# A two-layer decoder trunk: in the MLP's first iteration, casts move to GpSimd and modulation rows start one iteration later

## Chip, cores, metric

One core of one Trainium2 chip runs the whole trunk in one launch. The metric is the device time of one execution in microseconds (us), the median of several runs.

## The reference, cut to what matters

The trunk has two layers. Each has a mixer and then a squared-ReLU MLP, and each of these four sublayers is wrapped in the same way: normalise, scale and shift by rows computed from `c`, apply, normalise, gate, add. The change touches the two MLPs alone.

```python
def squared_relu_mlp(h, w1, w2):
    return jnp.square(jax.nn.relu(h @ w1)) @ w2          # (1024,1024) @ (1024,4096) @ (4096,1024)

def sandwich(x, c_act, sublayer, g_pre, g_post, w_mod, b_mod):
    shift, scale, gate = jnp.split(c_act @ w_mod + b_mod, 3, axis=-1)   # w_mod: 1024 x 3072
    h = rms_norm(x, g_pre) * (1 + scale[:, None]) + shift[:, None]
    return x + gate[:, None] * rms_norm(sublayer(h), g_post)
```

All data are float32, batch 1, 1024 tokens, width 1024.

## The kernel before

**Products in three passes.** A float32 operand is split into two parts: a "high" part, cast to the type fp32r, and a "low" part, the operand minus the high part. A product then takes three matmul passes (high x high, high x low, low x high). `split_w` (L153) makes both parts of a weight block of 128x1024: the cast runs on ScalarE (L160), the subtraction on VectorE (L162, both of its inputs in SBUF). If the counter `spare` is above zero, `split_w` takes one off it and casts on GpSimd instead (L158). `split_to` (L499) does the same for other operands: the cast on ScalarE (L500), the subtraction on VectorE (L501).

**The MLP's first product** (`h @ w1`) is done with seven products of half-size blocks in place of eight (Strassen's scheme in Winograd's form). Tokens are split in two halves, and the width and the hidden columns likewise. There are eight iterations `it` over hidden columns. Each loads four weight blocks x11, x12, x21, x22 (L579), forms sums of them on VectorE (L615 to L618, L628), and issues products number 1, 2, 4, 6, 7, 5, 3 in that order on TensorE (L547 to L549, called at L606 to L645), each with its own `split_w`. One iteration has 7 x 2 x 12 matmuls of 128x512. Six PSUM banks serve the products.

**Iteration 0 has more to do.** The first token half arrives in split form from the sublayer before. The second half is made inside iteration 0, after products 1 and 2, by `second_half` (L551). For each of four k it transposes two blocks on TensorE (L564), scales and shifts them on ScalarE (L566, L568), forms a high part's low part (L570) and four sums on VectorE (L571 to L574, two SBUF inputs each), and splits the four sums with `split_to` (L575, L576): 16 casts of 128x512 on ScalarE and 16 subtractions on VectorE. Products 4, 6, 7, 5 and 3 read these. Just before, the sublayer that precedes still finishes its last token tiles: `post` (L374: L380 to L390) and `pre_norm` (L367: square on ScalarE L370, mean on VectorE L133, power on GpSimd L135, scaling on VectorE L372), on which the transposes L564 wait.

**Modulation rows.** The queue `bgq` holds tasks that load 128 rows of `w_mod` (L285, a transfer issued on SyncE's queue) and accumulate them on VectorE (L287 for the first of eight, L289 for the others, 128x1024). Every eighth task also ends a row (`fin`: splits it, multiplies it with ones on TensorE, L306 or L323, and so on). In the MLP, each iteration but the first pops up to four tasks (L661 to L663). The first MLP has 24 tasks, so iterations 1 to 6 take them; the second has 8, taken in iterations 1 and 2.

**What sets the order.** Instructions are written in program order, but a planner then orders each engine's instructions by priority (earlier in the program goes first) and by the times at which it expects them to be ready. On the chip each engine runs its list strictly in that order, so an instruction that waits holds up everything behind it on its engine.

Of the kernel before, what the change touches and what calls it, by code (L numbers as in the profile page):

```python
# [28 lines left out]
def trunk(ctx: ExitStack, tc: tile.TileContext, x, c, rel_bias, norm_gains, mod_w, mod_b, mlp_w1, mlp_w2,  # L29
          e_w_in, e_conv_w, e_conv_b, e_dt_bias, e_A_log, e_D, e_ssd_norm, e_lambda, e_diff_norm, e_w_out,  # L30
          o_w_in, o_sinks, o_w_out, k_mat, k_onehot, k_mask, k_rope, k_ret, out, subs=(0, 1, 2, 3)):
    nc = tc.nc
# [27 lines left out]
    def turn(i):  # L60

        turns[i] = 1 - turns.get(i, 1)
        return turns[i]
# [87 lines left out]
    spare, lo_on = [0], [nc.vector]  # L151
# [262 lines left out]
    def new_hT(hf):  # L414
        return tuple(hp.tile([P, 8, 512], F32R, tag=f"{n}{hf}", name=f"{n}{hf}") for n in ("hh", "hl"))
# [80 lines left out]
                    hT[1] = make_hT(yp, 1, s + 1)  # L496
                return second

    def split_to(hi, lo, src):  # L499
        nc.scalar.copy(out=hi, in_=src)  # L500
        nc.vector.tensor_tensor(out=lo, in0=src, in1=hi.bitcast(F32), op=ALU.subtract)  # L501

    def mlp(yp, s):
# [13 lines left out]
        def bank():  # L517
            at[0] += 1
            return pg.tile([P, 512], F32, tag="g", name="pg") if at[0] % 6 < 2 else pw("pw")
# [3 lines left out]
        with ExitStack() as st:  # L523
            cp = st.enter_context(pool("c", 2))

            def block(tag):
                return cp.tile([P, 512], F32, tag=tag, name=tag)


            def pieces(i):  # L530
                return [slot(i + n, [P, 2, 512], F32R, "s") for n in range(2)]

            def of(t2):
                return lambda k: t2[k // 2][:, k % 2]

            def cols_of(t, k0):
                return lambda k: t[:, k0 + k]

            hh0, hl0 = hT[0]
            A = {1: (cols_of(hh0, 0), cols_of(hl0, 0)), 2: (cols_of(hh0, 4), cols_of(hl0, 4))}  # L540
# [10 lines left out]
            def second_half():  # L551
                a, b = mcol[s]
                hh1, hl1 = new_hT(1)
                A[4] = (cols_of(hh1, 4), cols_of(hl1, 4))
                A[7] = (cols_of(hh1, 0), cols_of(hl1, 0))
                for i, at_ in ((6, 8), (5, 4), (3, 0)):
                    A[i] = (of(pieces(at_)), of(pieces(at_ + 2)))
                for k in range(4):
                    a11, a12 = yp.whole[k], yp.whole[k + 4]
                    a2 = []  # L560
                    for kk, tag in ((k, "u3"), (k + 4, "c21")):
                        ps = pt.tile([P, 512], F32, tag="t", name="pht")
                        for i in range(4):
                            nc.tensor.transpose(ps[:, i * P:(i + 1) * P], yp.Y[4 + i][:, kk * P:(kk + 1) * P], ident)  # L564
                        a2.append(block(tag))
                        nc.scalar.activation(a2[-1], ps, AF.Identity, scale=a[:, kk:kk + 1], bias=b[:, kk:kk + 1])  # L566
                        if kk >= 4:
                            nc.scalar.activation(hh1[:, kk], ps, AF.Identity, scale=a[:, kk:kk + 1], bias=b[:, kk:kk + 1])  # L568
                    a21, a22 = a2
                    tt(out=hl1[:, k + 4], in0=a22, in1=hh1[:, k + 4].bitcast(F32), op=sub)  # L570
                    tt(out=a11, in0=a11, in1=a21, op=sub)  # L571
                    tt(out=a21, in0=a21, in1=a22, op=add)
                    tt(out=a22, in0=a22, in1=a11, op=sub)
                    tt(out=a12, in0=a12, in1=a22, op=sub)  # L574
                    for i, src in ((6, a22), (7, a11), (5, a21), (3, a12)):  # L575
                        split_to(A[i][0](k), A[i][1](k), src)  # L576

            def load(it):
                c0 = it * 256  # L579

                def src(j, r0, r1):
                    return w1[r0:r1, j * 2048 + c0:j * 2048 + c0 + 256].rearrange("(k p) n -> p k n", p=P)
                one = wp.tile([P, 8, 256], F32, tag="raw", name="raw", bufs=2)
                nc.sync.dma_start(out=one, in_=src(0, 0, D))
                if it == 0:
                    two = wp.tile([P, 8, 256], F32, tag="raw", name="raw", bufs=2)
                    nc.sync.dma_start(out=two, in_=src(1, 0, D))
                    two = [two[:, 0:4], two[:, 4:8]]
                else:
                    two = [slot(12 + i, [P, 4, 256], F32, "raw2") for i in range(2)]  # L590
                    for i in range(2):
                        nc.sync.dma_start(out=two[i], in_=src(1, i * 512, i * 512 + 512))
                return one[:, 0:4], two[0], one[:, 4:8], two[1]
# [3 lines left out]
            def square_relu(t, src):  # L597
                nc.scalar.activation(t, src, AF.Relu)
                nc.scalar.activation(t, t, AF.Square)

            for it in range(8):
                x11, x12, x21, x22 = load(it)
                pa, p1 = [bank(), bank()], [block("p1") for _ in range(2)]
                w = split_w(shape, x11)
                for g in range(2):
                    product(pa[g], 1, w, g, True, True)  # L606
                    nc.scalar.copy(out=p1[g], in_=pa[g])
                w = split_w(shape, x21)
                c11 = [block("c11") for _ in range(2)]
                for g in range(2):  # L610
                    product(pa[g], 2, w, g, False, True)
                    square_relu(c11[g], pa[g])
                if it == 0:
                    second_half()
                tt(out=x11, in0=x12, in1=x11, op=sub)  # L615
                t2 = slot(16, shape, F32, "t2")
                tt(out=t2, in0=x22, in1=x11, op=sub)
                tt(out=x21, in0=x21, in1=t2, op=sub)  # L618
                w = split_w(shape, x21)
                pe = [bank(), bank()]  # L620
                for g in range(2):
                    product(pe[g], 4, w, g, True, True)
                w = split_w(shape, t2)
                pb = [bank(), bank()]
                for g in range(2):
                    product(pb[g], 6, w, g, True, True)
                    tt(out=p1[g], in0=pb[g], in1=p1[g], op=add)
                tt(out=x12, in0=x22, in1=x12, op=sub)  # L628
                w = split_w(shape, x12)
                pc_ = [bank(), bank()]  # L630
                u3, c21 = [block("u3") for _ in range(2)], [block("c21") for _ in range(2)]
                for g in range(2):
                    product(pc_[g], 7, w, g, True, True)
                    tt(out=u3[g], in0=pc_[g], in1=p1[g], op=add)
                    tt(out=c21[g], in0=pe[g], in1=u3[g], op=add)
                    square_relu(c21[g], c21[g])
                w = split_w(shape, x11)
                pd = [bank(), bank()]
                for g in range(2):
                    product(pd[g], 5, w, g, True, True)  # L640
                    tt(out=u3[g], in0=pd[g], in1=u3[g], op=add)
                    square_relu(u3[g], u3[g])
                w = split_w(shape, x22)
                for g in range(2):
                    product(pd[g], 3, w, g, False, True)  # L645
                    tt(out=p1[g], in0=pd[g], in1=p1[g], op=add)
                    square_relu(p1[g], p1[g])
                sums = [slot(17 + i, [P, 2, 512], F32, "sums") for i in range(3)]
                for g in range(2):
                    kt = 2 * it + g  # L650
                    nc.sync.dma_start(out=ud[1][kt], in_=c11[g])
                    nc.sync.dma_start(out=ud[4][kt], in_=u3[g])
                    tt(out=sums[0][:, g], in0=c21[g], in1=u3[g], op=add)
                    tt(out=sums[1][:, g], in0=sums[0][:, g], in1=c11[g], op=sub)
                    tt(out=c21[g], in0=c11[g], in1=c21[g], op=sub)
                    nc.sync.dma_start(out=ud[7][kt], in_=c21[g])
                    tt(out=sums[2][:, g], in0=p1[g], in1=sums[1][:, g], op=sub)
                    nc.sync.dma_start(out=ud[2][kt], in_=p1[g])
                for i, n in ((5, 0), (6, 1), (3, 2)):
                    nc.sync.dma_start(out=ud[i][2 * it:2 * it + 2].rearrange("k p n -> p k n"), in_=sums[n])  # L660
                if it:  # L661
                    for _ in range(min(4, len(bgq))):
                        bgq.popleft()(slot(14 + turn(14), [P, D], F32, "mraw"))  # L663

# [939 lines left out]
```

## Time and profile before

| | us |
|---|---|
| median of 3 runs | 3015.42 |
| lowest, highest run | 3014.13, 3019.18 |
| the profiled execution, its device time | 3012.64 |
| its span, first to last instruction | 3010.7 |
| TensorE busy in the span | 2927.7 |
| VectorE busy | 1992.1 |
| ScalarE busy | 1320.9 |
| GpSimd busy | 443.5 |

The profile calls the engines PE (TensorE matmul), PEld (its weight load), DVE (VectorE), ACT (ScalarE), POOL (GpSimd) and SP (SyncE's queue). "L500" is line 500 of the kernel. PEclk is the granted TensorE clock as a share of full speed. The first MLP's iteration 0 lies at about 1084 to 1141 us of the span, the second one's about 1270 us later, with nearly the same times.

### The profile page before, as it was taken

The numbers are of one execution on the slowest core, as the hardware profiler recorded it, in microseconds if no ns is written. First come the engines' busy times: TensorE is split into PE (matmuls) and PEld (weight loads), VectorE is DVE, ScalarE is ACT, GpSimd is POOL, SyncE is SP. The second block draws the span as 40 slices with busy tenths as digits, with TensorE's granted clock in tenths as the row PEclk, the third lists the DMA queues.
The fourth block names the chain that finished last, engine by engine and source line by source line (L and its number), as shares of the span: only waits on it lengthen the run. The fifth ranks groups of instructions, "written<-read, shape, count | busy, mean of one in ns | idle before, by whom it ended". The sixth has DMA issues, their size and how long they took to land.

```text
span 3010.7 us, 39827 instructions
## 1 busy us (share of the span) xinstructions
PE 2927.7 (97%) x15250; PEld 2468.2 (82%) x15250; DVE 1992.1 (66%) x3175; ACT 1320.9 (44%) x2349; POOL 443.5 (15%) x368
## 2 busy tenths in 40 slices
PE   8999999999999989999999999999999899999998
PEld 5888888898877867888888878989988678888887
DVE  5677875766687578876646855565455876666476
ACT  5343335555453264445333545432222644454343
POOL 0244432213100120000000232001101200000021
PEclk9999999999999999999999999999999999999999
DMA  6211211312142146647737542153232454476464
GB/s 216 75 55 50 90 43 50 109 53 77 58 151 105 64 137 207 221 167 250 273 122 235 191 128 64 32 172 113 76 149 84 141 188 162 149 272 229 145 232 160
DMA packets 268320, 413.57 MB, mean 137 GB/s; under 512 B 14953, under 2 KB 150754, under 8 KB 267234
## 3 DMA queue, kind: packets, MB, share of 16 engines
q1 hardware_dynamic: 267744, 410.92, 40.6%
q8 instruction: 120, 1.97, 0.3%
q14 instruction: 70, 0.57, 0.1%
q10 hardware_dynamic: 386, 0.11, 0.0%
HBM read 319.23 MB, written 91.75 MB: 137 GB/s over the span
## 4 chain that ended last, share of the span: by engine, by line
PE 82%; DVE 9%; DMA 4%; ACT 2%; issue 2%; POOL 1%; SPq 0%; POOLq 0%; DVEq 0%; ACTq 0%
PE pw L730 5%; PE pw L731 5%; PE pw L732 5%; PE pg L444 4%; PE pg L445 4%; PE pg L446 4%; PE pw L547 4%; PE pw L549 4%; PE pw L548 4%; PE pg L798 4%; PE pg L799 4%; PE pg L800 4%; PE pg L456 3%; PE pg L458 3%; PE pg L457 3%; PE pg L730 2%
## 5 line engine op out<-in xcount | busy, mean ns | idle before, releaser
L160 ACT CAST wh<-raw 128x1024 fp32r<-128x1024 f32 (+1 forms) x218 | 227.6, 1047 | 292.7 <-PE pw L548 94.2
L444 PE MATMUL pg<-hh,wh 128*128 128x512 f32 x736 | 293.7, 399 | 3.8 <-ACT wh L160 2.7
L445 PE MATMUL pg<-hl,wh 128*128 128x512 f32 x736 | 291.0, 396 | 1.5 <-DVE hl L429 1.5
L446 PE MATMUL pg<-hh,wl 128*128 128x512 f32 x736 | 291.0, 395 | 0.3 <-DVE wl L162 0.3
L162 DVE TENSOR_TENSOR wl<-raw,wh 128x1024 fp32r<-128x1024 f32 (+1 forms) x162 | 199.5, 1232 | 135.2 <-ACT wh L160 127.9
L798 PE MATMUL pg<-wh,hh 128*128 128x256 f32 (+1 forms) x960 | 280.0, 292 | 5.2 <-DVE zs L833 3.2
L800 PE MATMUL pg<-wh,hl 128*128 128x256 f32 (+1 forms) x960 | 276.6, 289 | 0.6 <-DVE hl L429 0.6
L799 PE MATMUL pg<-wl,hh 128*128 128x256 f32 (+1 forms) x960 | 276.7, 288 | 0.5 <-DVE wl L162 0.5
L500 ACT CAST u<-uraw 128x1024 fp32r<-128x1024 f32 x112 | 117.1, 1048 | 293.5 <-PE pw L731 174.3
L501 DVE TENSOR_TENSOR u<-uraw,u 128x1024 fp32r<-128x1024 f32 x112 | 141.2, 1262 | 153.8 <-ACT u L500 153.4
L731 PE MATMUL pw<-wl,u 128*128 128x512 f32 x608 | 240.3, 395 | 0.0
L730 PE MATMUL pw<-wh,u 128*128 128x512 f32 x608 | 240.1, 396 | 0.0
L732 PE MATMUL pw<-wh,u 128*128 128x512 f32 x608 | 239.4, 394 | 0.0
L798 PEld LDWEIGHTS pg<-wh,hh 128*128 128x128 f32 x960 | 185.4, 193 | 7.6 <-DVE zs L833 2.7
L162 POOL TENSOR_TENSOR wl<-raw,wh 128x1024 fp32r<-128x1024 f32 x58 | 145.3, 2510 | 289.2 <-ACT wh L160 260.1
L799 PEld LDWEIGHTS pg<-wl,hh 128*128 128x128 f32 x960 | 185.2, 193 | 2.2 <-DVE wl L162 0.8
L800 PEld LDWEIGHTS pg<-wh,hl 128*128 128x128 f32 x960 | 184.8, 193 | 2.1 <-DVE hl L429 1.3
L456 PE MATMUL pg<-wh,u 128*128 128x512 f32 x448 | 181.7, 406 | 2.2 <-DVE u L935 1.4
L458 PE MATMUL pg<-wh,u 128*128 128x512 f32 x448 | 177.6, 397 | 0.0
L457 PE MATMUL pg<-wl,u 128*128 128x512 f32 x448 | 177.3, 396 | 0.0
L444 PEld LDWEIGHTS pg<-hh,wh 128*128 128x128 f32 x736 | 139.0, 189 | 33.3 <-ACT wh L160 3.2
L445 PEld LDWEIGHTS pg<-hl,wh 128*128 128x128 f32 x736 | 139.0, 189 | 29.1 <-DVE hl L429 2.0
(402 smaller groups left out, 7233.8 us busy)
## 6 DMA issues: line engine op xcount, KB each, us to landing
x<-in_mlp_w_dram SPq DMA_DIRECT2D x128, 512.0 KB, 7.1
uraw<-ud SPq DMA_DIRECT2D x56, 1024.0 KB, 5.6
mraw<-in_mod_w_dram SPq DMA_DIRECT2D x64, 512.0 KB, 4.7
ud<-sums SPq DMA_DIRECT2D x48, 512.0 KB, 3.8
raw<-in_mlp_w_dram SPq DMA_DIRECT2D x18, 1024.0 KB, 5.4
raw<-in_e_w_in_dram SPq DMA_DIRECT2D x32, 512.0 KB, 3.9
ud<-c SPq DMA_DIRECT2D x64, 256.0 KB, 3.1
raw<-in_mlp_w_dram SPq DMA_DIRECT2D x28, 512.0 KB, 4.6
```

The source lines that it names most:

```text
L162: lo_on[0].tensor_tensor(out=wl, in0=src, in1=wh.bitcast(F32), op=ALU.subtract)
L444: mm(ps, lhsT=wh[:, k], rhs=hh[:, k], start=(k == 0), stop=False)
L445: mm(ps, lhsT=wh[:, k], rhs=hl[:, k], start=False, stop=False)
L446: mm(ps, lhsT=wl[:, k], rhs=hh[:, k], start=False, stop=(k == 7))
L456: mm(ps, lhsT=uh[:, tl], rhs=wh[:, f % 2], start=(f == 0), stop=False)
L458: mm(ps, lhsT=ul[:, tl], rhs=wh[:, f % 2], start=False, stop=(f == 3))
L730: mm(ps[t], lhsT=uh[:, k, ts], rhs=wh[:, k], start=b, stop=False, **on)
L731: mm(ps[t], lhsT=uh[:, k, ts], rhs=wl[:, k], start=False, stop=False, **on)
L732: mm(ps[t], lhsT=ul[:, k, ts], rhs=wh[:, k], start=False, stop=e, **on)
L798: mm(ps[:, 0:n], lhsT=hh[:, k, tl], rhs=wh[:, i], start=(k == 0), stop=False)
L799: mm(ps[:, 0:n], lhsT=hh[:, k, tl], rhs=wl[:, i], start=False, stop=False)
L800: mm(ps[:, 0:n], lhsT=hl[:, k, tl], rhs=wh[:, i], start=False, stop=(k == 7))
```

## The change

Three edits. First, `split_to` gets an argument for the cast's engine, and `second_half` passes GpSimd: the 16 casts of the four sums, per MLP, go from ScalarE to GpSimd. Second, after `second_half` the counter `spare` is set to 3: the next three `split_w` calls (the blocks of products 4, 6 and 7, in iteration 0 alone) cast on GpSimd. Third, the modulation tasks start in iteration 2 in place of 1.

```diff
-    def split_to(hi, lo, src):
-        nc.scalar.copy(out=hi, in_=src)
+    def split_to(hi, lo, src, cast=nc.scalar.copy):
+        cast(out=hi, in_=src)
         nc.vector.tensor_tensor(out=lo, in0=src, in1=hi.bitcast(F32), op=ALU.subtract)
...
                     for i, src in ((6, a22), (7, a11), (5, a21), (3, a12)):
-                        split_to(A[i][0](k), A[i][1](k), src)
+                        split_to(A[i][0](k), A[i][1](k), src, nc.gpsimd.tensor_copy)
...
                 if it == 0:
                     second_half()
+                    spare[0] = 3
                 tt(out=x11, in0=x12, in1=x11, op=sub)
...
-                if it:
+                if it >= 2:
                     for _ in range(min(4, len(bgq))):
                         bgq.popleft()(slot(14 + turn(14), [P, D], F32, "mraw"))
```

## Rows read from the trace of the kernel before

**Rows 1.** The page, part 1: busy us, share of the span, instructions

```profile
PE 2927.7 (97%) x15250; PEld 2468.2 (82%) x15250; DVE 1992.1 (66%) x3175; ACT 1320.9 (44%) x2349; POOL 443.5 (15%) x368
```

**Rows 2.** Busy time by stretch: start:end, length, then engines, clock, DMA

```profile
core 0: us, PE busy (x) PEld busy (x) DVE busy (x) ACT busy (x) POOL busy (x), PEclk, DMA share, GB/s
1091.30:1105.50 14.20, 6.43 (x20) 4.52 (x19) 13.01 (x20) 9.69 (x15) 1.99 (x3) 0.66 0.35 112
1114.20:1132.70 18.50, 17.48 (x84) 14.03 (x83) 18.35 (x29) 15.80 (x25) 0.00 (x0) 1.00 0.55 187
1091.30:1132.70 41.40, 32.57 (x138) 25.74 (x137) 37.05 (x58) 32.00 (x50) 1.99 (x3) 0.84 0.38 128
2361.00:2402.40 41.40, 32.52 (x139) 25.68 (x137) 37.03 (x58) 32.01 (x50) 1.99 (x3) 0.84 0.38 128
1135.00:1170.00 35.00, 33.55 (x142) 26.51 (x143) 32.56 (x39) 14.68 (x22) 0.00 (x0) 1.00 0.71 237
1170.00:1205.00 35.00, 35.00 (x154) 28.61 (x154) 22.93 (x28) 17.29 (x25) 0.00 (x0) 1.00 0.53 176
```

**Rows 3.** Waits of PE, 1085 to 1135 us: total us, times, longest

```profile
PE pht L564 <- DVE Y L372: 6.3, 2, 4.5
...
PE pw L548 <- DVE s L501: 1.0, 1, 1.0
```

**Rows 4.** Chain of waits, 1097 to 1106 us: start, us, what

```profile
1097.98 0.93 DVE xt L388
...
1100.53 3.40 DVE wl L162 x3
...
1104.73 0.76 DVE Y L372
...
1105.54 0.48 PE pht L564
```

**Rows 5.** Instructions in order, all engines, 1131.9 to 1132.8: start, us, [idle before <-releaser]

```profile
1131.98 0.69 DVE L501 TENSOR_TENSOR s<-c,s 128x512 fp32r<-128x512 f32 x1
...
1132.72 0.50 PE L548 MATMUL pw<-s,wh 128*128 128x512 f32 x1 [1.05 <-DVE s L501]
```

**Rows 6.** Instructions in order, POOL, 1075 to 1110 us

```profile
1074.88 1.30 POOL L383 TENSOR_TENSOR yg<-Y,gg 128x512 f32<-128x512 f32 x1 [2.26 <-DVE Y L465]
...
1081.59 1.67 POOL L383 TENSOR_TENSOR yg<-Y,gg 128x512 f32<-128x512 f32 x1 [2.82 <-DVE Y L465]
```

**Rows 7.** Instructions in order, DVE, 1080 to 1102 us

```profile
1081.43 0.68 DVE L429 TENSOR_TENSOR hl<-whole,hh 128x512 fp32r<-128x512 f32 x1
1082.03 2.32 DVE L162 TENSOR_TENSOR wl<-raw,wh 128x1024 fp32r<-128x1024 f32 x1
...
1100.44 1.22 DVE L162 TENSOR_TENSOR wl<-raw,wh 128x1024 fp32r<-128x1024 f32 x1
1101.58 1.22 DVE L162 TENSOR_TENSOR wl<-t,wh 128x1024 fp32r<-128x1024 f32 x1
```

**Rows 8.** Line 158, GpSimd's casts: count, ns min/median/max, first and last start

```profile
L158 POOL CAST wh<-raw x2: 1046/1166/1285, 1734.0 to 1735.4; 128x1024 fp32r<-128x1024 f32 x2
```

**Rows 9.** Instructions in order, DVE, 1725 to 1745 us

```profile
1733.08 1.27 DVE L409 SCALAR_TENSOR_TENSOR xt<-low,rs,xt 128x1024 f32<-128x1024 f32 x1
```

**Rows 10.** Line 500, ScalarE's casts: count, ns min/median/max

```profile
L500 ACT CAST s<-u x8: 605/626/637, 1108.6 to 2396.9; 128x512 fp32r<-128x512 f32 x8
```

**Rows 11.** Waits of PE, 1135 to 1400 us

```profile
PE pw L547 <- DVE p L627: 1.1, 1, 1.1
PE pw L547 <- ACT p L607: 0.9, 1, 0.9
```

**Rows 12.** Modulation rows (tile mraw), 1100 to 1440 us: count, ns min/median/max

```profile
L289 DVE SCALAR_TENSOR_TENSOR macc<-mraw,cact,macc x21: 1277/1283/1286, 1141.9 to 1287.5; 128x1024 f32<-128x1024 f32 x21
L287 DVE TENSOR_SCALAR macc<-mraw,cact x3: 748/750/750, 1136.7 to 1255.4; 128x1024 f32<-128x1024 f32 x3
```

**Rows 13.** Waits of SP's queue, 1100 to 1440 us

```profile
SPq L743 <- PE pmc L323: 10.5, 1, 10.5
```

## The prediction

> **What bounds the kernel now.** I read the page first: PE is busy for 2927.7 of 3010.7 us [rows 1], so an edit beside PE can win only where PE stands still or runs at its lower clock. Then the stretches around the two places that the change touches. Both MLPs show the same picture (41.40 us long, all engines within 0.1 us of each other) [rows 2], so I work out one MLP and double it. In this stretch PE is busy for only 32.57 of 41.40 us, and its granted clock is 0.84, in the first 14.2 us even 0.66 of 2.4 GHz, so part of it at 1.2 GHz. This is where time can be won. Third, who makes PE wait: DVE, with 6.3 us for L372 and 1.0 us for L501 [rows 3]. Fourth, DVE itself: 37.05 of 41.40 us busy, and in the second part, where the four sums are made and split, 18.35 of 18.50; ACT has 15.80 there, POOL nothing [rows 2]. So **DVE is the bound of this stage**, and ACT, which the change relieves, has spare time. The chain of waits says the same: through L388, three L162, L372 to the transpose L564 [rows 4].
>
> The end of this stage I call T: the subtraction L501 that finishes the last k of product 6 ends at 1132.67, and PE, which has stood for 1.05 us, starts 0.05 us later [rows 5]. Products 5 and 3 have to wait for PSUM banks that product 6 still holds, so there is nothing else for PE to do: from T on, a delay of DVE is a delay of PE, with no slack.
>
> **Part 1: 16 casts of 128x512 from ACT to POOL.** ACT loses 16 x 0.626 = 10.0 us [rows 10]; as ACT isn't the bound, this by itself gives little. What it costs depends on whether POOL and DVE can work at once. The rows say no: a POOL multiplication L383 takes 1.30 us alone. One that starts at 1081.59, while a DVE subtraction runs until 1082.11, takes 1.67 and ends at 1083.26, 1.15 after the subtraction's end; and the DVE subtraction L162 that starts at 1082.03 takes 2.32 instead of 1.22, ending 1.09 after POOL's end [rows 6, 7]. They take turns. Each turn hides 0.15 us of POOL's own time (1.30 - 1.15), and DVE's 1.09 stands against a spacing of 1.14 when L162 follow each other (1100.44 to 1101.58) [rows 7], another 0.05. For a cast there is one row: two of 128x1024 took 1046 and 1285 ns, the first of them started at about 1733.97, beside a DVE instruction that ran until 1734.35 [rows 8, 9]. The cast that ran beside it is thus the longer one, and 1734.35 plus 0.9 is where it ends: a cast with one input waits as well.
>
> The Trainium skill says so as a rule, on its page "SBUF — State Buffer", section "Who interferes with whom": a DVE instruction with two SBUF inputs contends with a GpSimd instruction that reads SBUF, and one blocks the other fully. By that rule all subtractions and sums of this stage are hit, and the casts with them. The two rows of L383 and L162 agree (2.32 against 1.22 us); that a cast holds DVE up, no row here shows.
>
> The price of a 128x512 cast on POOL has no row. Half of 1046 is 0.52, ACT's own takes 0.626 [rows 8, 10]. I take 0.62, since such instructions have a fixed part, less the 0.20 that turns hide: 0.42 us of DVE's time per cast. The bounds are 0.32 and, with nothing hidden, 0.62; nothing below zero, since no DVE instruction goes away. 15 of the 16 lie before T: **6.3 us** (4.8 to 9.3). The Trainium skill's "GPSIMD Engine Reference", section 3.1, has a figure for a best case of 512 elements, 769 ns; by it the sum would be 15 x 0.57 = 8.5 us, an estimate. The row for 1024 elements (1.05 us) speaks against it.
>
> **Part 2: three casts of 128x1024 to POOL.** They are 1.05 us each on either engine [rows 8], on POOL less 0.20: **2.6 us** of DVE's time (2.1 to 3.1). They gain something: in DVE's list, three L162 (3.40 us) stand ahead of the mean L133 and the scaling L372 of the last token tile, on which PE waits 4.5 us [rows 3, 4]. With casts that come later, the planner may put the last tile ahead. But the three L162 belong to products 4, 6 and 7 and are still needed before T, on the engine that bounds T; moving them saves no DVE time, it only fills DVE's idle time. POOL's list has the power L135 in the same chain; a wide cast ahead of it holds it up by up to 1.05 us.
>
> **What idle time can take up.** DVE stands for 41.40 - 37.05 = 4.35 us in the stretch [rows 2]. Part of this is latency of the last tile's chain (ACT, DVE, POOL, DVE in turn) and stays. I take 3.0 us as filled, between 0 and 4.35. T comes 6.3 + 2.6 - 3.0 = **5.9 us later**, and PE with it.
>
> **Part 3: modulation rows one iteration later.** Four tasks leave iteration 1: one L287 and three L289, 0.75 + 3 x 1.28 = 4.6 us of DVE [rows 12], out of a stretch where DVE is busy 32.56 of 35 us into ones with 22.93 of 35 [rows 2]. PE's two stalls there, 1.1 and 0.9 us [rows 11], could shrink; but DVE arrives some 6 us late with the same work. I take 0.9 us back, between 0 and 2.0. The four transfers L285 per iteration leave SP's queue too, where stores and the next weight loads stand behind them; nothing on PE waits for SP, so I put this at nothing. At the far end, the first MLP's last task now ends in iteration 7, and its `fin` takes one of the two buffers that the second product's loads L743 need; before, such a load waited 10.5 us for it without PE noticing [rows 13]. Cover: these loads are issued 20 to 30 us ahead. I take zero, 4 us once if the cover is too short. In the second MLP 8 tasks move to iterations 2 and 3, at no cost.
>
> **The clock.** The stretch before T already has half-speed windows after PE's stalls. A longer stall at T may bring one more, which costs PE up to 2 us; if the stall of 4.5 us shrinks, as much may come back. I take zero, plus or minus 2.
>
> **Sum.** Per MLP 5.9 - 0.9 = 5.0 us, for both 10.0. Against the profiled execution's own 3012.64 us that is 3022.6. This execution lies 2.8 us below the median of 3015.42, which is what I forecast on: 3015.4 + 10.0 = **3025.4 us**. Ends per MLP: low 4.8 + 2.1 - 4.35 - 2.0 - 2 = -1.5; high 9.3 + 3.1 + 2 = 14.4 (and 4 once). Both ends at once are unlikely; the forecast's own range is +2 to +11 per MLP, 3019 to 3037.
>
> **Rivals.**
> *A, faster: a cast on POOL hardly holds DVE up.* Only one row shows a POOL cast beside DVE, and it shows the cast waiting, not DVE. Then DVE loses nothing, 3 us of its idle time go, and up to 2 us of stalls in iteration 1 [rows 11]: 4 us per MLP, 3007. It decides at the point where the 18 casts together cost DVE less than 3.0 + 0.9 = 3.9 us, 0.22 each. For it speaks that a POOL instruction with one input may need less of what the two share; against it that the cast waited in full.
> *B, no change:* the casts cost what I say, but the idle time takes up 4.35, the last tile's chain is 1 to 2 us earlier with its half-speed window gone, and iteration 1 gives back 2.0: 8.9 - 4.35 - 2.0 - 2 = 0.6 per MLP, 3016.6.
> *C, much slower:* POOL's list runs strictly in order. If wide casts stand ahead of L135, and DVE's next subtraction often waits for its own cast, nothing overlaps: 9.3 + 3.1 = 12.4 per MLP, 3040.
> That the edit doesn't do what it says I exclude: the counter is used by the next three `split_w`, which are those of products 4, 6 and 7.
>
> **How the numbers follow.** A measurement of this kernel can tell about 0.2%, 6 us, from no change. Forecast 0.50 (of it 0.06 within 6 us), A 0.22, B 0.18, C 0.10. Slower by over 0.2%: 0.44 + 0.10 = 0.54. Same: 0.06 + 0.18 = 0.24, faster 0.22. The range leaves out the better half of A (below 3006) and the worse part of C (above 3039).
>
> **What would show it.** In the changed profile: L500 on POOL 32 times, at 0.6 us and up to 1.2 where DVE runs; the subtractions and sums L501 and L570 to L574 at 1.0 to 1.2 us where a cast is running, against 0.68; DVE's stretch from L571 of the first k to T longer by 4 to 6 us; a wait of PE for L501 of some 5 to 7 us in place of 1.0. The step fails if these DVE instructions keep 0.68 us (then A), or if PE waits no longer at T although they don't. If PE's wait for L372 falls from 6.3 us by more than 3, the planner's new order has given more than I allow.

## The result and the profile after

The changed kernel takes **3040.42 us** (median of 4 runs, 3036.49 to 3045.66); the kernel before, run beside it, 3014.78 (4 runs). The ratio is 1.0089, 95% interval [1.0074, 1.0104]: 25.6 us slower. Forecast were 10 us and 3025.4, with a range that ends at 3037 for the forecast itself and at 3039 with the rivals; the direction was right, the size too small by 15.6 us. The profiled execution took 3042.54 us, its span is 3040.8. From line 615 on, a line of the changed kernel has a number higher by one.

The page, part 1, as in [rows 1]:

```profile
PE 2935.7 (97%) x15250; PEld 2472.4 (81%) x15250; DVE 2008.7 (66%) x3175; ACT 1298.6 (43%) x2311; POOL 489.4 (16%) x406
```

PE is busy 8 us longer in a span that is 30.1 us longer: most of the loss is time in which PE stands.

To find where, I took the start of the same instruction in both traces, found by line and operands, and followed the difference along time. It grows in each MLP's first iteration, by 13.3 and 13.5 us. The rest, +5.3 us in the first layer's mixer and -2.4 in the second's, lies in code that the change doesn't touch; there the granted clock differs from one execution to the next (in the 50 us from 1750 of the kernel before it is 0.97, in the same code after 1.00, which takes 2 us less there; the profile of "rows alone" below stands at -2.8 behind the first layer's mixer, not at +5.3). So the profiled pair shows 30.1 us and the medians show 25.6.

Busy time by stretch, the kernel after; the first two stretches end at the same events as the two of 41.40 us in [rows 2], the last L465 and T, in the first and the second MLP; the third begins just behind T:

```profile
core 0: us, PE busy (x) PEld busy (x) DVE busy (x) ACT busy (x) POOL busy (x), PEclk, DMA share, GB/s
1095.63:1150.60 54.97, 34.54 (x138) 25.65 (x138) 50.45 (x62) 21.32 (x32) 25.11 (x22) 0.83 0.34 115
2377.53:2432.92 55.39, 35.76 (x138) 26.61 (x137) 50.46 (x62) 20.84 (x31) 25.13 (x22) 0.81 0.34 114
1153.00:1188.00 35.00, 35.00 (x147) 28.39 (x147) 27.51 (x33) 15.09 (x22) 0.00 (x0) 0.96 0.82 262
```

In [rows 2] the stretch lasted 41.40 us. Now it lasts 54.97 and 55.39, so T comes 13.6 and 14.0 us later, where the forecast said 5.9. DVE's busy time went from 37.05 to 50.45, +13.4, and DVE's idle time stayed (4.35, now 4.52). The count tells more: 62 instructions of DVE against 58 (each count has one that only reaches into the end of the stretch). Longer instructions alone would not add any; **DVE does work ahead of T that was behind T before**.

Waits of PE, the kernel after, 1090 to 1160 us (total us, times, longest), against [rows 3]:

```profile
PE pht L564 <- DVE Y L372: 9.2, 2, 6.8
PE pw L548 <- DVE s L501: 4.7, 2, 4.2
PE pg L548 <- DVE hl L501: 2.7, 1, 2.7
PE pw L548 <- DVE hl L570: 2.2, 2, 1.5
```

L372 costs 2.9 us more than before, and L501 and L570 cost 7.4 and 2.2, together 9.6, in place of 1.0 for L501.

**The price of one turn.** Lines 500 and 574 of the kernel after: count, ns min/median/max, first and last start:

```profile
L500 POOL CAST hh<-whole x8: 610/817/1069, 1114.2 to 2414.1; 128x512 fp32r<-128x512 f32 x8
L500 POOL CAST s<-u x8: 1013/1042/1137, 1115.5 to 2418.3; 128x512 fp32r<-128x512 f32 x8
...
L574 DVE TENSOR_TENSOR whole<-whole,c x8: 1091/1092/1093, 1117.5 to 2421.1; 128x512 f32<-128x512 f32 x8
```

and line 574 of the kernel before:

```profile
L574 DVE TENSOR_TENSOR whole<-whole,c x8: 682/684/689, 1110.7 to 2401.0; 128x512 f32<-128x512 f32 x8
```

A cast that waits for nothing takes 0.61 us (the shortest, 610 ns), one that has to wait for DVE about 1.01. The DVE sum L574, 0.68 us before, takes 1.09 each time: +0.41. In each MLP 16 of the 36 DVE instructions of the four k are about that long (0.98 to 1.15 us), 6.5 us in all. So what no row of before showed is shown now: a cast on POOL holds DVE up. This agrees with the Trainium skill, page "SBUF — State Buffer", section "Who interferes with whom", for an instruction with two SBUF inputs beside a GpSimd instruction that reads SBUF.

**The order.** DVE's list in the kernel after, up to T (start, us, instruction, [idle before <-releaser]):

```profile
1138.47 1.09 DVE L574 TENSOR_TENSOR whole<-whole,c 128x512 f32<-128x512 f32 x1
1139.48 1.21 DVE L162 TENSOR_TENSOR wl<-raw,wh 128x1024 fp32r<-128x1024 f32 x1
1140.62 1.09 DVE L501 TENSOR_TENSOR hl<-whole,hh 128x512 fp32r<-128x512 f32 x1
1141.63 0.68 DVE L501 TENSOR_TENSOR s<-c,s 128x512 fp32r<-128x512 f32 x1
1144.12 1.22 DVE L162 TENSOR_TENSOR wl<-raw,wh 128x1024 fp32r<-128x1024 f32 x1 [1.81 <-ACT wh L160]
1145.27 0.68 DVE L501 TENSOR_TENSOR s<-whole,s 128x512 fp32r<-128x512 f32 x1
1145.87 1.22 DVE L616 TENSOR_TENSOR raw<-raw,raw 128x1024 f32<-128x1024 f32 x1
1147.01 0.68 DVE L501 TENSOR_TENSOR s<-u,s 128x512 fp32r<-128x512 f32 x1
1147.61 1.22 DVE L618 TENSOR_TENSOR t<-raw,raw 128x1024 f32<-128x1024 f32 x1
1148.74 1.22 DVE L629 TENSOR_TENSOR raw<-raw,raw 128x1024 f32<-128x1024 f32 x1
1149.88 0.68 DVE L501 TENSOR_TENSOR s<-c,s 128x512 fp32r<-128x512 f32 x1
```

The cast that the last of these needs is the POOL row:

```profile
1138.01 1.01 POOL L500 CAST s<-c 128x512 fp32r<-128x512 f32 x1 [1.21 <-DVE c L573]
```

and PE, which waits for the last one, starts here:

```profile
1150.62 0.80 PE L548 MATMUL pw<-s,wh 128*128 128x512 f32 x1 [4.24 <-DVE s L501]
```

The cast is ready at 1139.02, the subtraction runs at 1149.88. In between stand four other subtractions L501, two splits L162, and L616, L618 and L629, which are weight sums of **iteration 1**. The second split, too, is of iteration 1: it is the sixth L162 from product 4's on, and iteration 0 has only five left. DVE waits 1.81 us for that split's ScalarE cast, and the subtraction at T stands behind it. In the kernel before the three sums and this split, the four instructions more, stood behind T (1132.67):

```profile
1130.11 0.62 ACT L500 CAST s<-c 128x512 fp32r<-128x512 f32 x1
...
1132.58 1.22 DVE L162 TENSOR_TENSOR wl<-raw,wh 128x1024 fp32r<-128x1024 f32 x1
...
1135.52 1.22 DVE L615 TENSOR_TENSOR raw<-raw,raw 128x1024 f32<-128x1024 f32 x1
```

From the end of the cast to T I call the lag: 11.5 and 11.3 us here, 1.9 before (1130.73 to 1132.67).

The clock changes too. Busy time of the kernel after around T (columns as above):

```profile
1142.00:1156.00 14.00, 9.76 (x24) 6.93 (x24) 12.15 (x15) 2.09 (x2) 0.00 (x0) 0.63 0.41 116
```

The granted clock is 0.63 on average, part of the stretch at 1.2 GHz, as PE stood for 2.71 us ahead of 1141.77 and for 4.24 ahead of 1150.62. In [rows 2] the stretch from 1135 on had 1.00.

### The profile page after: what moved, and what is told of

The parts are those of the page before. It is cut to its first block, busy times and chain, and to the rows that moved or that the text cites. A ratio compares the mean times of both kernels' runs of the same rounds, so it can differ in the third digit from the quotient of the medians.

```text
span 3040.8 us, 39833 instructions
## 1 busy us (share of the span) xinstructions
PE 2935.7 (97%) x15250; PEld 2472.4 (81%) x15250; DVE 2008.7 (66%) x3175; ACT 1298.6 (43%) x2311; POOL 489.4 (16%) x406
## 5 line engine op out<-in xcount | busy, mean ns | idle before, releaser
L162 DVE TENSOR_TENSOR wl<-raw,wh 128x1024 fp32r<-128x1024 f32 (+1 forms) x162 | 198.3, 1225 | 158.5 <-ACT wh L160 157.5
L500 ACT CAST u<-uraw 128x1024 fp32r<-128x1024 f32 x112 | 116.8, 1048 | 276.9 <-PE pw L732 172.6
L501 DVE TENSOR_TENSOR u<-uraw,u 128x1024 fp32r<-128x1024 f32 x112 | 139.7, 1251 | 144.2 <-ACT u L500 142.4
L162 POOL TENSOR_TENSOR wl<-raw,wh 128x1024 fp32r<-128x1024 f32 x58 | 145.2, 2507 | 290.3 <-ACT wh L160 259.6
```

The source lines that it names most:

```text
L162: lo_on[0].tensor_tensor(out=wl, in0=src, in1=wh.bitcast(F32), op=ALU.subtract)
```

## The experiments

**How they are read.** For each kernel the table has the shift against the kernel before, first/second MLP, in us: A from the last L465 to the first L571; B from there to T; C from T to a cast L500 some 30 casts into the second product; the lag; and the medians (difference to the kernel before on the same chip, ratio and its interval). A, B and C are of one traced execution for each kernel, so the medians decide on the time.

| kernel | A | B | C | lag | median, ratio |
|---|---|---|---|---|---|
| before | | | | 1.9 / 1.9 | |
| after | +2.2 / +2.2 | +11.3 / +11.8 | +0.7 / -0.5 | 11.5 / 11.3 | +25.6, 1.0089 [1.0074, 1.0104] |
| small casts alone | 0 / 0 | +11.9 / +10.9 | -2.1 / -1.9 | 11.3 / 11.3 | +22.2, 1.0076 [1.0058, 1.0094] |
| wide casts alone | +2.2 / +2.2 | +0.8 / -0.1 | -0.4 / -0.2 | 1.9 / 1.9 | +2.6, 1.0006 [0.9996, 1.0017] |
| rows alone | 0 / 0 | -0.2 / -0.2 | +4.4 / -0.2 | 1.9 / 1.9 | +5.0, 1.0019 [1.0010, 1.0028] |
| all casts, rows as before | +2.2 / +2.6 | +11.4 / +9.0 | -0.8 / +0.5 | 11.3 / 8.4 | +30.8, 1.0102 [1.0081, 1.0123] |
| after, wide order by hand | +2.3 / +2.2 | +4.1 / +3.9 | +6.4 / +2.7 | 4.0 / 4.0 | +20.9, 1.0071 [1.0055, 1.0087] |
| before, extra copies | 0 / 0 | +5.0 / +4.9 | -0.6 / +0.8 | 3.5 / 3.5 | +9.3, 1.0034 [1.0021, 1.0047] |
| before, last tile first | -1.1 / -1.1 | -1.5 / -0.5 | -0.7 / +1.3 | 2.3 / 2.6 | -5.3, 0.9984 [0.9975, 0.9994] |
| before, wide order by hand | 0 / 0 | -1.4 / -1.5 | +4.4 / +4.4 | 0.7 / 0.7 | +8.3, 1.0031 [1.0021, 1.0042] |
| after, narrow order by hand | +2.2 / +2.2 | +5.0 / +5.2 | +2.2 / +0.5 | 4.0 / 4.0 | +14.4, 1.0050 [1.0038, 1.0062] |
| before, narrow order by hand | 0 / 0 | -1.0 / -0.3 | +4.4 / +1.1 | 0.7 / 0.7 | -0.5, 0.9999 [0.9990, 1.0007] |
| after, half of the small casts | +2.2 / +2.2 | +3.6 / +4.2 | +2.4 / +0.9 | 2.9 / 2.9 | +11.9, 1.0037 [1.0022, 1.0051] |

### The parts of the change, one at a time

Small casts alone: the kernel before with

```diff
-                        split_to(A[i][0](k), A[i][1](k), src)
+                        split_to(A[i][0](k), A[i][1](k), src, nc.gpsimd.tensor_copy)
```

> The 16 casts of the four sums alone go to GpSimd; the three wide casts stay on ScalarE and the modulation rows start in iteration 1, as before. Theory 'turns' (that of the prediction: a cast only lengthens the VectorE instruction beside it by 0.4 us): 15 x 0.42 us less some 2 us of idle time = 4 us per MLP, 3023 us. Theory 'order' (the planner, which takes a GpSimd cast for late, also puts the subtraction that ends product 6 behind sums of iteration 1 in VectorE's list; in the changed kernel's profile it runs 7.6 us after the subtraction could have): 4 + 6 to 8 us per MLP, 3035 to 3039 us, nearly the whole loss of the change.

Measured +22.2 us: nearly the whole loss, and all of it between L571 and T, with the long lag. This is near what 'order' expected and far from 'turns'.

Wide casts alone: the kernel before with

```diff
                     second_half()
+                    spare[0] = 3
```

> The three wide casts alone go to GpSimd (counter at 3); the 16 small ones stay on ScalarE, rows as before. Theory 'turns': 2.6 us of VectorE's time per MLP, taken up by its idle time, 0 +- 2 us per MLP, 3011 to 3019 us. Theory 'list': GpSimd's list is strict, the power for the last token tile stands behind wide casts, PE's wait for L372 grows from 6.3 to some 9 us per MLP, 2 to 3 us per MLP, 3019 to 3021 us.

Measured +2.6 us, not told from no change. The traces still show where it acts: the last tile's chain is 2.2 us later in each MLP, the same as in the kernel after. How, POOL's list of the kernel after shows:

```profile
1099.57 2.48 POOL L158 CAST wh<-raw 128x1024 fp32r<-128x1024 f32 x1 [6.83 <-DVE raw L619]
1101.99 1.50 POOL L158 CAST wh<-t 128x1024 fp32r<-128x1024 f32 x1
1103.45 2.12 POOL L135 TENSOR_TENSOR rs<-ms,expo 128x1 f32<-128x1 f32 x2
1105.53 1.67 POOL L158 CAST wh<-raw 128x1024 fp32r<-128x1024 f32 x1
1109.85 1.41 POOL L135 TENSOR_TENSOR rs<-ms,expo 128x1 f32<-128x1 f32 x1 [2.66 <-DVE ms L133]
```

and DVE's list of the kernel after beside it:

```profile
1106.22 2.05 DVE L388 SCALAR_TENSOR_TENSOR xt<-yg,rs,xt 128x1024 f32<-128x1024 f32 x1
...
1109.63 1.23 DVE L162 TENSOR_TENSOR wl<-raw,wh 128x1024 fp32r<-128x1024 f32 x1
1111.30 0.75 DVE L372 TENSOR_SCALAR Y<-xt,rs 128x1024 f32<-128x1024 f32 x1 [0.44 <-POOL rs L135]
```

Two wide casts stand ahead of the powers L135. The third holds L388 up (2.05 us against 1.28 before). The last power takes 1.41 us beside L162, where it took 0.55 in the kernel before beside an idle DVE:

```profile
1104.14 0.55 POOL L135 TENSOR_TENSOR rs<-ms,expo 128x1 f32<-128x1 f32 x1 [5.68 <-DVE ms L133]
```

In exchange one of the three L162 of [rows 4] now runs while that power does, behind the last mean L133: the kind of gain that the prediction thought possible. But two of them stand ahead of L388 now, and the net is a loss.

Rows alone: the kernel before with

```diff
-                if it:
+                if it >= 2:
```

> Only the modulation rows move, from iterations 1 to 6 to iterations 2 to 7 (second MLP: 2 and 3); all casts as before. Prediction's step: 0.9 us per MLP back, 3013 us. Rival: PE's two stalls in iteration 1 (2.0 us per MLP) go, 3011 us. Rival: the row that now ends in iteration 7 holds a buffer that the second product's loads need, PE stalls there by up to 4 us once, 3017 us.

Measured +5.0 us. Waits of PE in this kernel, 1135 to 1400 us, against 0.9 in [rows 11]:

```profile
PE pw L547 <- ACT p L607: 3.3, 2, 1.9
```

Waits of ACT in the same stretch, this kernel and the kernel before:

```profile
ACT p L607 <- DMA ud<-p: 17.3, 9, 4.6
...
ACT p L607 <- DMA ud<-p: 14.1, 8, 3.6
```

The copy L607 writes a block that the last iteration's stores still read. These stores go through SP's queue, and PE waits for L607: in the kernel before for 0.9 us at 1164.92, here for 1.9 at 1162.87 and for 1.4 at 1322.40. The 2.4 us more of waiting are half of the 4.4 us in C; the clock, 0.86 in the 10 us from 1165, is most of the rest. That the later rows bring this about is not shown. The control with the narrow order, further below, has its rows as before and no loss by its medians, and its trace shows the same picture in the same place, with C at +4.4:

```profile
PE pw L547 <- ACT p L610: 2.5, 1, 2.5
```

PE's wait of 1.1 us for DVE [rows 11], which the prediction hoped to shrink, is still there (1.14 us at 1131.99), and the stall in the second product that the third rival named is not to be seen. So the loss of 5.0 us is measured, its cause is open.

All casts, rows as before: the changed kernel without the third edit.

> The changed kernel with the rows back in iterations 1 to 6: both groups of casts on GpSimd. If the later rows give VectorE room where it comes late (prediction's step, 0.9 us per MLP): 3042 us. If they give up to 4.6 us per MLP, since VectorE is further behind than was thought: up to 3049 us. If they do nothing: 3040 us.

Measured +30.8 us. The casts are the loss. What the rows do beside them can't be told: by the medians the changed kernel, with its later rows, is 5.2 us faster than this one, but the two intervals overlap; by the traces it loses 1.5 us more per MLP (A, B and C together).

### Turns against order

Extra copies: the kernel before, ScalarE casts and all, with 16 more casts on POOL whose result nothing reads:

```diff
                         split_to(A[i][0](k), A[i][1](k), src)
+                        nc.gpsimd.tensor_copy(out=gg[:, i % 2 * 512:i % 2 * 512 + 512].bitcast(F32R), in_=src)
```

> The kernel before, casts on ScalarE, plus 16 casts of the same four sums on GpSimd whose result is not read (it goes over a tile whose next value is written later). Nothing waits for them, so VectorE's list stays as before; the turns alone are left. Turns: VectorE's instructions beside them take 1.09 in place of 0.68 us, PE comes later by 15 x 0.41 us less 2 us of idle time = 4 us per MLP, 6 to 9 us above the kernel before in all. If GpSimd's casts don't hold VectorE up: no difference. If the whole loss of the small casts were turns: 20 us.

Measured +9.3 us. Line 574 of this kernel:

```profile
L574 DVE TENSOR_TENSOR whole<-whole,c x8: 678/1092/1094, 1111.3 to 2407.2; 128x512 f32<-128x512 f32 x8
```

Nearly the same turns (14 long DVE instructions per MLP where the changed kernel has 16), no subtraction that depends on POOL, no DVE instruction more ahead of T, and T is 5.0 and 4.9 us later, not 11: **turns alone cost what the prediction said** (4 to 6 us from L571 to T); the rest must come from elsewhere.

Wide order by hand: in iteration 0 all from product 5's split on, and the whole of iteration 1 up to its last product, is issued after the subtraction at T. As an edit of the changed kernel, and as a control in the kernel before:

```diff
+                if it == 0: behind.enter_context(tc.issue_after(low[6].ins))
                 w = split_w(shape, x11)
...
+                if it == 1: behind.close()
                 sums = [slot(17 + i, [P, 2, 512], F32, "sums") for i in range(3)]
```

> The changed kernel, with VectorE's list set by hand at one place: in iteration 0, what belongs to products 5 and 3, and all of iteration 1, comes behind the subtraction that ends product 6 (low part of the last k). GpSimd's casts stay. Theory 'order': this subtraction then runs about 7 us earlier in each MLP, the time is 12 to 15 us below the changed kernel's, 11 to 14 us above the kernel before. Theory 'turns alone' (the casts' turns on VectorE explain it all, the order is a symptom): at most 3 us below the changed kernel.

> The kernel before with the same order set by hand as in e5_order, all casts on ScalarE and rows as before: what this order is worth by itself. In the kernel before the subtraction already runs as soon as it can, so no difference, within 3 us. If it is faster by 5 us or more, the gain of e5_order is not that of an order that the GpSimd casts spoiled.

In the changed kernel B falls by 7.2 and 7.9 us, but C grows by 5.7 and 3.2, and the time falls by 4.7 us alone, which neither theory had. The control shows why, against its own expectation (within 3 us): with ScalarE casts this order costs 8.3 us by itself, as product 5's split comes late. Waits of PE in the control, 1085 to 1160 us:

```profile
PE pg L549 <- DVE wl L162: 2.7, 1, 2.7
```

The two differ by 12.6 us, 6.3 per MLP. So the casts cost little more than the prediction had (10.0 in all), once the order is the same on both sides; but this order, written by hand, is too coarse to show what the changed kernel loses by the planner's.

Narrow order by hand: only the four weight sums of iteration 1 and product 3's split of iteration 0 are issued after the subtraction at T; again with a control.

```diff
+            def sums_after(it):
+                return tc.issue_after(low[6].ins) if it == 1 else ExitStack()
...
+                with sums_after(it):
                     tt(out=x11, in0=x12, in1=x11, op=sub)
                     tt(out=t2, in0=x22, in1=x11, op=sub)
                     tt(out=x21, in0=x21, in1=t2, op=sub)
...
+                with tc.issue_after(low[6].ins) if it == 0 else ExitStack():
                     w = split_w(shape, x22)
```

> The changed kernel in full, with a smaller order written by hand than in e5_order: only the four weight sums of iteration 1 and product 3's weight split of iteration 0 are issued after the subtraction that T names; product 5's split stays where the planner puts it. In the changed kernel three of those sums (3 x 1.13 us) and waits of DVE stand ahead of that subtraction, which runs 10.9 us after its cast. Theory (about half of the loss is order, half is taking turns on the memory port): T falls back by 4 to 7 us per MLP, and product 5's split is not late as in e5_order, so nothing is paid after T: 8 to 14 us below the changed kernel, 3026 to 3032. Rival (the loss is the turns alone and the late place in the list only follows from DVE having no time): T stays where it is, within 2 us per MLP of the changed kernel, 3037 to 3042. Second rival (whatever is put behind T is paid there): T is 7 us earlier, but PE waits as much longer after it, 3036 to 3042.

> The kernel before with the same smaller order by hand as e9_sums, casts on ScalarE and rows as before. In the kernel before the sums of iteration 1 already stand behind T, so the order should change little there: within 4 us of the kernel before if it is free (then e9_sums less this kernel is the casts' price with the order held, 10 to 14 us); 4 to 9 us above it if product 3's split, put behind T, is late as in e8_control.

Measured 3028.0 us, +14.4, and the control -0.5: by the medians this order costs nothing by itself that can be told (its interval reaches from -3.0 to +2.1 us), and the changed kernel gets 11.2 us (25.6 less 14.4) back from it, 10.7 of them more than the control. The 14.9 us between the two are the casts' price, and the rows', with the order the same on both sides. The end of DVE's list up to T, the changed kernel with the narrow order:

```profile
1140.68 0.68 DVE L501 TENSOR_TENSOR s<-whole,s 128x512 fp32r<-128x512 f32 x1
1141.28 0.68 DVE L501 TENSOR_TENSOR s<-u,s 128x512 fp32r<-128x512 f32 x1
1141.89 0.68 DVE L501 TENSOR_TENSOR s<-c,s 128x512 fp32r<-128x512 f32 x1
1142.49 2.35 DVE L162 TENSOR_TENSOR wl<-raw,wh 128x1024 fp32r<-128x1024 f32 x2
```

Busy time from the last L465 to T, both MLPs, the changed kernel with the narrow order and then the control (columns as above):

```profile
1093.99:1142.60 48.61, 35.85 (x138) 27.02 (x137) 44.73 (x57) 20.84 (x31) 24.61 (x22) 0.79 0.32 108
2373.48:2422.30 48.82, 33.94 (x138) 25.40 (x137) 44.71 (x57) 20.86 (x31) 24.62 (x22) 0.83 0.32 108
...
1090.34:1130.74 40.40, 31.81 (x138) 25.34 (x138) 35.83 (x57) 30.89 (x49) 1.99 (x3) 0.83 0.39 130
2362.06:2403.18 41.12, 31.04 (x138) 24.53 (x137) 35.85 (x57) 30.79 (x49) 2.00 (x3) 0.88 0.38 127
```

No sum of iteration 1 stands ahead of T any more. T is 7.2 and 7.4 us later than before, half of 13.6 and 14.0, with all 16 turns still there (6.5 us). The rival that the long lag only followed from a DVE without time falls. Part of this gain is product 3's split (1.14 us), which stands ahead of T in the kernel before and which this order puts behind it: in the control T is 1.0 and 0.3 us earlier than before. Against the control, with the same 57 DVE instructions in the stretch, T is 8.2 and 7.7 us later.

### Why the planner does it: argued, not shown

Half of the small casts: the changed kernel, with the casts for products 6 and 5 on POOL and those for 7 and 3 on ScalarE.

```diff
-                        split_to(A[i][0](k), A[i][1](k), src, nc.gpsimd.tensor_copy)
+                        split_to(A[i][0](k), A[i][1](k), src, nc.gpsimd.tensor_copy if i in (6, 5) else nc.scalar.copy)
```

> The changed kernel, but of the 16 casts per MLP only the 8 for products 6 and 5 are on GpSimd, the other 8 stay on ScalarE. Theory (the planner reckons GpSimd's casts longer than they are, so its list of 16 runs late in the planner's reckoning and the subtractions are put behind other work): with 8 casts there is no such backlog; the subtraction at T follows its cast by 4 us or less (1.9 before, 11.5 after), 8 turns cost 3.3 us per MLP, the wide casts 2.2 as before, and T is 4 to 6 us later than in the kernel before, 3022 to 3027. Rival (any subtraction that hangs on a GpSimd cast is put late, however few they are): the lag stays at 8 us or more and T is 10 us or more later, 3032 to 3038.

Measured 3026.78 us, +11.9. The subtraction at T hangs on a POOL cast here as well, yet the lag is 2.9 us, and the sums of iteration 1 stand behind it (DVE's list of this kernel):

```profile
1134.01 0.68 DVE L501 TENSOR_TENSOR s<-c,s 128x512 fp32r<-128x512 f32 x1
1134.62 0.68 DVE L501 TENSOR_TENSOR s<-whole,s 128x512 fp32r<-128x512 f32 x1
1135.22 1.21 DVE L616 TENSOR_TENSOR raw<-raw,raw 128x1024 f32<-128x1024 f32 x1
```

So a dependency on POOL alone is not enough; it takes more of the casts there (that it is their number, and not which of them, one kernel can't show). This fits a planner that reckons POOL's casts longer than they are and sees a backlog with 16 of them: in the list of the kernel after the subtractions from 1145.27 to T stand 1.74 and 2.87 us apart with weight sums put between, though their casts had been ready for some time (the last of them for 10.9 us). The planner's own times were not read, so the backlog is argued from this one dose, not shown.

### A faster version

Last tile first: in the kernel before, the three L162 of products 4, 6 and 7 in iteration 0 are issued after the last tile's L372.

```diff
+                if it == 0: behind.enter_context(tc.issue_after(normed.ins))
                 w = split_w(shape, x21)
+                if it == 0: behind.close()
```

> The kernel before, with one place of VectorE's list set by hand: the three L162 of products 4, 6 and 7 in iteration 0 come behind the last token tile's L372. If VectorE bounds the stage, only its idle time can be won: PE's wait for L372 falls by 2.9 us, the end of product 6 comes 1 to 2.3 us earlier, 2 to 5 us per run below the kernel before. If PE's wait itself counted: 6 us below. If neither: the same.

Measured 3008.41 us, 5.3 us below the kernel before, ratio 0.9984 [0.9975, 0.9994]: faster than both kernels, with the casts left on ScalarE. Waits of PE, 1085 to 1135 us, against 6.3 and 1.0 in [rows 3]:

```profile
PE pht L564 <- DVE Y L372: 3.3, 2, 1.8
...
PE pw L548 <- DVE s L501: 1.6, 1, 1.6
```

Of 3.0 us that PE waits less for L372, 1.1 remain by the first L571.

## Why the prediction was right or wrong

- **What bounds the stage: right.** DVE is the bound, ACT's relief gave nothing (ACT busy 32.00 to 21.32 us in the stretch, no gain), and from T on a delay of DVE is a delay of PE: C is small in the kernel after.
- **Part 1, the price of a turn: right.** 0.61 us for a cast alone (0.62 forecast), 0.41 of DVE's time for each (0.42), 16 turns and 6.5 us per MLP (15 and 6.3). The figure of 769 ns that the Trainium skill's "GPSIMD Engine Reference", section 3.1, has for a best case of 512 elements is too long for this cast: 610 ns.
- **Part 2, the wide casts: size right, way in part different.** Alone they lengthen DVE's work ahead of T by 2.4 us against 2.6 forecast, and T comes 3.0 and 2.1 us later. Part of this comes by way of the power L135 in the last tile's chain, which the prediction named and priced at up to 1.05, but did not add.
- **"I take 3.0 us as filled": wrong.** With the same order on both sides the casts add 8.9 us to DVE's work ahead of T (44.73 against 35.83), which is the prediction's own 6.3 + 2.6. But DVE's idle time falls only from 4.57 to 3.88 us in the first MLP and from 5.27 to 4.11 in the second: 0.7 and 1.2 filled. So T comes 8.2 and 7.7 us later, not 5.9. The last tile's chain got longer (A, +2.2), so there was little for the casts to hide in.
- **The order of DVE's list: the step that failed.** The prediction asked what the planner would do with the three L162 and the last tile, where it could gain, and took the rest of the list as given. There is no term for what the planner does with 16 subtractions whose inputs now come from another engine. Its size is B after less B with the narrow order, 6.3 and 6.6 us, less the 1.0 and 0.3 that this order gives the control: 5.3 and 6.3 us per MLP. Of the medians it is 10.7 us, most of the 15.6 that are missing. The other 4.9 are what the casts cost above the 10.0 with the order held (14.9); the idle time that was not filled, some 2 us per MLP, and the 0.9 us per MLP that the rows were to give back are of that size. Two signs that the prediction named told it: PE's wait for L501, "some 5 to 7 us", was 7.4, and the stretch from L571 to T, "longer by 4 to 6 us", grew by 11.3.
- **Part 3, the rows: not borne out, small.** 0.9 us per MLP back was forecast; alone the edit costs 5.0 us in all, and beside the casts neither a gain nor a loss could be told. "Nothing on PE waits for SP" was false in the kernel before already: PE's 0.9 us for L607 [rows 11] is a wait for a store in SP's queue. Whether that makes the 5.0 us stays open.
- **The clock: about its size.** There is a half-speed window after T, and PE's busy time in the stretch is 2.0 and 3.2 us longer, where 2 were allowed. DVE sets T, so not all of this is lost; behind T, C is +0.7 and -0.5.
- **Rival C gave 3040, and 3040.4 was measured, but not by its mechanism: the match is luck.** It had every cast at the full 0.62 us because DVE waits for its own cast. DVE's instructions pay 0.41, and in its list the cast is long done when the subtraction starts. What came true of it is the power behind the wide casts. **Rival A** (a cast hardly holds DVE up) falls with L574's 1.09 us, **rival B** with the idle time that wasn't filled.

## What to carry to other kernels

When a producer moves to another engine, price two things on the engine that consumes: what each instruction loses beside the new neighbour, and where the planner will now put the consumers; look at what stands directly behind the critical one in its list, for that is what slipped ahead of it here (the next iteration's split and sums). If a move must be made, hold the order by hand at the fewest instructions that do it, and run the same order in the kernel before: the wide one cost 8.3 us by itself, the narrow one nothing that could be told. An engine that isn't the bound is not worth relieving at the expense of the one that is.

## What the runs showed of the hardware

- A POOL instruction can wait through more than one DVE instruction. The first wide cast ran from 1099.57 to 1102.05, 2.48 us against 1.04 for the shortest, while DVE issued three two-input instructions back to back (1099.26, 1099.86, 1100.46) that kept their 0.68 us.
- Size is no protection. The power L135, 128x1, took 1.41 us beside an L162 and 0.55 beside an idle DVE. Both of its inputs are in SBUF.
